# Two transformer blocks in one kernel: the first block's residual and norms on other engines, and one more slot for split weights

## The chip, the core and the metric

The kernel runs on one core of a Trainium2 chip. The metric is device time in microseconds, from one launch, as the median of three runs. A core has five engines with a queue of instructions each: TensorE (PE: products; PEld: its weight loads), VectorE (DVE), ScalarE (ACT), GpSimd (POOL) and SyncE (SP), on whose queue nearly all transfers are issued. Each engine works through its queue in order, and semaphores tie the queues together. TensorE's clock is granted at one of two levels, 2.4 GHz (1.00 in the profile's rows) or 1.2 GHz (0.50).

## What is computed

256 tokens of 1024 features, in float32, through two blocks of two layers each. The first block's layer is, twice:

```python
shift, scale, gate = ada_modulation(c, ada_w[layer, 0], ada_b[layer, 0])
h = x * (1.0 + scale) + shift
y = mixer_ab(h, ...) if layer % 2 == 0 else mixer_c(h, ...)
x = layer_norm(DN_ALPHA * x + gate * y, ln_g[layer, 0], ln_b[layer, 0])
shift, scale, gate = ada_modulation(c, ada_w[layer, 1], ada_b[layer, 1])
h = x * (1.0 + scale) + shift
y = squared_relu_mlp(h, mlp_w1[layer], mlp_w2[layer])
x = layer_norm(DN_ALPHA * x + gate * y, ln_g[layer, 1], ln_b[layer, 1])
```

So it has four halves (mixer, MLP, mixer, MLP), each of which ends in a layer norm of alpha x + gate y, with alpha the fourth root of 4. The second block (a gated recurrence, an MLP, latent attention, an MLP) has plain residual sums and RMS norms in place of it.

## The kernel before, in words

**Products.** A float32 product is made of three: each operand is cut into a high part (rounded) and a low part (the rest), and hi x hi, hi x lo and lo x hi are summed in PSUM (`mmA` at L219, `mmB` at L233; their lines L222 to L224 and L236 to L238 carry nearly all of TensorE's time). Tokens are in two tiles of 128, `t` = 0 and 1.

**Weights.** `Stream` holds all weights as items of 128 x 2048 float32 (1 MB) in the order of their use. A load (L122, on SP's queue) goes into one of four `raw` buffers. An item is then split in four pieces of 512 columns: ScalarE writes `whi` (L152), VectorE writes `wlo` = raw - whi (L153). The parts go into rings of `HL` = 6 tiles of 1024 columns each, which is room for three items. `hold` (L100) names items whose VectorE pieces are queued only behind a given instruction. Items of the adaLN modulation are in the stream as well: VectorE multiplies and sums them (`junk`, L421).

**MLP.** 16 hidden blocks; block j needs the items `(name, 1, j)` and `(name, 2, j)`. In the first block's two MLPs the first products of the blocks j = 0 and 1 run token tile by token tile (`head=2`), so that they can begin on tile 0.

**Between two halves** (`build`, L1684 to L1697; called a transition below). The last products of a half are held back in `fin(t)` (`tail`, L613). For each tile, `post_ln` (L533) does on VectorE: gate times y (L541), plus alpha x (L542), statistics (L543, L545); then the reciprocal root on GpSimd (L245, tile `rs`); then the normalized `xh`, two VectorE instructions of 128 x 512 (L551). `to_xT` (L270) transposes `xh` on TensorE (L279), ScalarE applies gain, scale and shift (L289), VectorE makes the high part `xTh` (L291) and the low part `xTl` (L292), with which the next half's products begin. After both tiles, `residual` (L594) makes alpha (xh g + b) for the next norm, on GpSimd: two instructions of 128 x 1024 a tile (L599, L600), into a new tile `xa`. `load_gb` (L581) loads the rows g and b; GpSimd multiplies them by alpha (L590, L591) except for the last norm. GpSimd also multiplies the first input by alpha (L1010), early in the kernel. `bcast_diag` (L436) puts a gate on all partitions.

**Order.** The program names engines and data; a planner with a cost model then puts each engine's instructions in an order, by the place in the program and by what it takes to be ready, and adds the semaphores. So what runs beside a transition may come from a later line of the program. A tile pool that opens after another has closed reuses its memory.

The four transitions: T0 (first mixer to first MLP, about 140 to 175 us of the profile), T1 (first MLP to second mixer, 340 to 380), T2 (second mixer to second MLP, 480 to 515), T3 (second MLP to the second block, 680 to 715).

Of the kernel before, what the change touches and what calls it, by code (L numbers as in the profile page):

```python
# [52 lines left out]
class Weights:  # L53
    """A chunk's hi and lo parts, in tiles that end at `cuts`"""
# [18 lines left out]
class Native:  # L73
    """A chunk as it is, in two tiles that meet at `cut`"""
# [10 lines left out]
class Stream:  # L85
    """Weights in the order of their use: loads run ahead, parts are split ahead."""

    def __init__(self, kb, load_ahead):
        self.kb = kb
        self.items = []  # L90
        self.index = {}
        self.nload = 0
        self.load_ahead = load_ahead
        self.queue = []
        self.nsplit = 0
        self.res = {}
        self.raw = {}
        self.held, self.behind = (), ()

    def hold(self, key, a, b, behind):  # L100
        """Items a to b after `key` are split behind these instructions"""
        i = self.index[key]
        self.held, self.behind = range(i + a, i + b), [x.ins if hasattr(x, "ins") else x for x in behind]

    def add(self, key, src, cols, cuts=None, gains=None, fn=None, step=512, f32=False):
        self.index[key] = len(self.items)
        self.items.append((key, src, cols, gains, fn, step, cuts, f32))

    def _load_to(self, i):
        kb = self.kb  # L110
        while self.nload <= min(i, len(self.items) - 1):
            key, src, cols = self.items[self.nload][:3]
            if self.items[self.nload][7]:
                # float32 products: into the split parts' place
# [11 lines left out]
    def _pieces(self, i):  # L126
# [17 lines left out]
        for a, b, g in gains:  # L144
            def pc(a=a, b=b, g=g):
                i, s = w.at(slice(a, b))
                if i == len(his):
                    his.append(kb.pw.tile([128, kb.HW], F32R, tag="whi", name=kb.nm("whi"), bufs=kb.HL))
                    los.append(kb.pw.tile([128, kb.HW], F32R, tag="wlo", name=kb.nm("wlo"), bufs=kb.HL))
# [12 lines left out]
    def pump(self, n=1, limit=None):  # L162
        """Emit up to n pieces; at most to item `limit`."""
# [28 lines left out]
class Kern:  # L192
# [33 lines left out]
    def mm(self, ps, x, w, c, start, stop):  # L226
        """x (hi, lo) with split weights, or one float32 operand with weights as they are"""
# [12 lines left out]
    def rsqrt(self, out, in_, mul, eps, n=1, pool=None):  # L240
        """out = (in * mul + eps) ** -0.5 on [128, n]"""
# [9 lines left out]
    def tm(self, name):  # L251
        """Token-major [128, 1024] scratch."""
        return self.px.tile([128, 1024], F32, tag="tm", name=self.nm(name), bufs=8)

    def split_evac(self, hi, lo, ps, gain=None):
        """hi + lo = ps (* gain), ps in PSUM"""
# [13 lines left out]
    def to_xT(self, x, t, xT, mode):  # L270
        """One token-major tile -> its columns of the feature-major hi/lo tiles.
        mode: None, (gain columns,) or (scale columns, bias columns)"""
# [54 lines left out]
    def setup_late(self):  # L327
        """Masks and rope tables"""
        nc, A, pc, c = self.nc, self.aps, self.pc, self.c
        nc.sync.dma_start(self.sink, A["rows"][ROWS["sinks"]:ROWS["sinks"] + 1, 0:8].to_broadcast([128, 8]))  # L330
        # bf16 identity and masks (added to the scores in PSUM)
# [13 lines left out]
        # rope tables of the second block: [cos | cos], [-sin | sin]  # L345
# [4 lines left out]
    def rope1_tables(self):  # L350
        """cos/sin of positions * inv, one [128, 64] each per token tile, sin signed [-sin | sin]."""
# [23 lines left out]
        # cos(r) = sin(r + pi/2), wrapped into [-pi, pi]  # L375
# [18 lines left out]
    def rope(self, out, src, nh, cos, sin):  # L394
        """out, src: [128, nh * 64]; src in PSUM"""
# [19 lines left out]
    def ada_piece(self, raw, j, acc, n):  # L415
        """acc[:, n] = sum_k raw[:, j, k] * silu(c)[k]"""
# [8 lines left out]
    def ada_bias(self, mod, acc, i, a, b):  # L425
        """mod = acc + b (+1 on scale and gate)"""
        self.nc.vector.tensor_tensor(mod[:, a:b], acc[:, a:b], self.adab[:, 24 * i + a:24 * i + b], op=ALU.add)

    def diag(self, cols):
        """Eight columns, each on the diagonal of a 128 x 128 block"""  # L430
# [5 lines left out]
    def bcast_diag(self, dst, d):  # L436
        """dst[128, 1024] = the blocks' diagonals along the free axis, on every partition"""
        nc = self.nc
        for g in range(2):
            p = self.ps("o")  # L440
            nc.tensor.matmul(p, self.ones, d[:, 4 * g:4 * g + 4, :].rearrange("p a b -> p (a b)"), start=True, stop=True)
            nc.scalar.activation(dst[:, g * 512:(g + 1) * 512], p, AF.Copy)

# [1 line left out]
    def attn_scores(self, t, heads, qk, mask, scale, sink=None, norm_act=False):  # L445
        """Scores and softmax of a few heads of one query tile.
        t = 0: 4 heads x 128 keys; t = 1: 2 heads x 256 keys.  Returns P (token-major)."""
# [43 lines left out]
    def attn_T(self, pt):  # L491
        """Transposed probabilities: four [128 keys, 128 queries] blocks."""
# [8 lines left out]
    def attn_pv(self, t, heads, pT, v, o, split=True):  # L501
        """o(h): PSUM region of head h; v(h, block): [128 keys, dv]"""
# [4 lines left out]
        elif split:  # L507
            # two column halves of the array side by side
# [10 lines left out]
    def attention(self, units, lag=2, hook=None):  # L519
        """units: list of (stage1 -> P, stage2(pT))"""  # L520
# [12 lines left out]
    def post_ln(self, acc, gate, xa, t):  # L533
        """One token tile: normalized alpha x + gate y, without the gain"""
# [12 lines left out]
        self.rsqrt(rs, ag[:, 1:2], 1.0, LN_EPS)  # L547
        x = self.tm("xh")
        for nb in range(2):
            sl = slice(nb * 512, nb * 512 + 512)  # L550
            self.ln_last = nc.vector.tensor_scalar(x[:, sl], r[:, sl], ag[:, 0:1], rs,  # L551
                                                   op0=ALU.subtract, op1=ALU.mult)
        return x

    def norm_in(self, li, gate):
        """Norm of layer half li and the next half's input, to be called for one token tile after the other"""
# [24 lines left out]
    def load_gb(self, li, scale):  # L581
        """Gain and bias rows of a norm on every partition, scaled"""
# [6 lines left out]
        if scale != 1.0:  # L589
            nc.gpsimd.tensor_scalar(g, g, scale, None, op0=ALU.mult)  # L590
            nc.gpsimd.tensor_scalar(b, b, scale, None, op0=ALU.mult)  # L591
        self.gb = (g, b)

    def residual(self, x):  # L594
# [1302 lines left out]
```

## Time and profile before

| | us |
|---|---|
| median of 3 runs | 1391.0 |
| lowest, highest run | 1390.44, 1391.79 |
| span of the profiled execution | 1393.9 |

The profiled execution gives no time of its own outside the span: from its first to its last instruction it took 1393.9 us, 2.9 us above the median of the timed runs. The page's table of engines has the busy time, the share of the span and the instructions of each engine. A row of the view by stretches gives the length of a stretch, then the busy time of PE, PEld, DVE, ACT and POOL with the instructions that began in it, TensorE's granted clock, the share of the transfer engines and GB/s. A row of the timeline gives start, length, engine, line, operation, out<-in with shapes, and how many instructions were merged; in brackets the idle time before, and who ended it. Consecutive instructions of one engine overlap by some 0.08 us.

### The profile page before, as it was taken

Reading aid. Unit: us, or ns where it says so; the run is one execution under the profiler, and the core shown is the slowest. Engines: PE = TensorE matmul, PEld = TensorE weight load, DVE = VectorE, ACT = ScalarE, POOL = GpSimd, SP = SyncE. Lnnn points to the kernel's source line nnn. Section 1 sums busy time; section 2 is a strip of 40 time slices with the busy share of each in tenths; the row PEclk is TensorE's granted clock in tenths of the full one; section 3 lists DMA queues with packets and bytes.
Section 4 is the critical chain, followed back from the end, with each engine's and each line's share of the span. In section 5 each row is a group of like instructions: output and inputs, shape, how many; then the busy total and the mean of one; then the engine's idle time right before and its main releaser. Section 6 shows DMA issues by size and latency. Waiting matters only on the chain.

```text
span 1393.9 us, 20506 instructions
## 1 busy us (share of the span) xinstructions
PE 1315.7 (94%) x7816; PEld 1114.9 (80%) x7822; DVE 987.2 (71%) x1862; ACT 697.4 (50%) x1490; POOL 110.1 (8%) x98
## 2 busy tenths in 40 slices
PE   5979799999799979999889999999999999999997
PEld 2446599988687669998679897999987987899996
DVE  7799898866998688555688787555558555655554
ACT  2257445544466445445453445444457764544552
POOL 3001400000400130000030000000001000000000
PEclk9989899999899989999979999999999999999999
DMA  9549398774375348555343423555544342355540
GB/s 367 218 159 354 103 373 320 286 276 152 127 296 214 119 138 315 184 185 179 119 168 118 152 92 121 181 181 181 184 168 177 122 151 92 136 182 187 191 166 31
DMA packets 38837, 260.16 MB, mean 187 GB/s; under 512 B 4562, under 2 KB 4818, under 8 KB 9171
## 3 DMA queue, kind: packets, MB, share of 16 engines
q1 hardware_dynamic: 38594, 258.34, 51.0%
q8 instruction: 61, 1.00, 0.3%
q0 software_dynamic: 144, 0.52, 0.1%
q14 instruction: 38, 0.30, 0.1%
HBM read 257.79 MB, written 1.05 MB: 186 GB/s over the span
## 4 chain that ended last, share of the span: by engine, by line
PE 80%; DVE 12%; issue 3%; ACT 2%; DMA 1%; POOL 1%; SPq 0%; DVEq 0%; POOLq 0%; ACTq 0%
PE acc L224 13%; PE acc L222 12%; PE acc L223 12%; PE scr L237 9%; PE scr L238 9%; PE scr L236 9%; DVE wlo L153 3%; PE scr L458 3%; DVE xh L551 1%; DMA raw<-in_ada_dram 1%; DVE junk L421 1%; PE o L496 1%; PE acc L1294 1%; PE o L1294 1%; POOL sm L245 1%
## 5 line engine op out<-in xcount | busy, mean ns | idle before, releaser
L153 DVE TENSOR_TENSOR wlo<-raw,whi 128x512 fp32r<-128x512 f32 x724 | 490.2, 710 | 287.4 <-ACT whi L152 274.5
L152 ACT ACTIVATE whi<-raw 128x512 fp32r<-128x512 f32 x724 | 421.5, 626 | 455.3 <-PE acc L224 202.6
L236 PE MATMUL scr<-xTh,whi 128*128 128x256 f32 x1088 | 310.5, 286 | 1.9 <-DVE xTh L291 1.9
L237 PE MATMUL scr<-xTl,whi 128*128 128x256 f32 x1088 | 309.2, 284 | 0.4 <-DVE xTl L292 0.2
L238 PE MATMUL scr<-xTh,wlo 128*128 128x256 f32 x1088 | 309.2, 284 | 0.0
L236 PEld LDWEIGHTS scr<-xTh,whi 128*128 128x128 f32 x1088 | 208.9, 192 | 5.2 <-DVE xTh L291 2.4
L237 PEld LDWEIGHTS scr<-xTl,whi 128*128 128x128 f32 x1088 | 209.0, 192 | 3.9 <-DVE xTl L292 0.9
L238 PEld LDWEIGHTS scr<-xTh,wlo 128*128 128x128 f32 x1088 | 209.1, 192 | 0.1
L222 PE MATMUL acc<-whi,hh 128*128 128x512 f32 x512 | 202.1, 395 | 0.0
L224 PE MATMUL acc<-whi,hl 128*128 128x512 f32 x512 | 201.8, 396 | 0.0
L223 PE MATMUL acc<-wlo,hh 128*128 128x512 f32 x512 | 201.7, 395 | 0.0
L421 DVE SCALAR_TENSOR_TENSOR junk<-raw,csil 128x1024 bf16<-128x1024 f32 x96 | 121.5, 1265 | 8.9 <-DMA raw<-in_ada_dram 7.9
L224 PEld LDWEIGHTS acc<-whi,hl 128*128 128x128 f32 x512 | 96.5, 188 | 22.9 <-DVE hl L695 0.8
L222 PEld LDWEIGHTS acc<-whi,hh 128*128 128x128 f32 x512 | 96.8, 189 | 20.4 <-ACT hh L693 1.1
L223 PEld LDWEIGHTS acc<-wlo,hh 128*128 128x128 f32 x512 | 96.5, 189 | 19.6
L245 POOL TENSOR_TENSOR sm<-rsq,mhalf 128x1 f32<-128x1 f32 (+2 forms) x26 | 19.7, 757 | 869.1 <-DVE rsq L244 869.1
L222 PE MATMUL acc<-whi,xTh 128*128 128x512 f32 (+1 forms) x176 | 67.0, 382 | 3.6 <-DVE xTh L291 3.6
L223 PE MATMUL acc<-wlo,xTh 128*128 128x512 f32 (+1 forms) x176 | 66.0, 375 | 2.0 <-DVE wlo L153 2.0
L224 PE MATMUL acc<-whi,xTl 128*128 128x512 f32 (+1 forms) x176 | 65.4, 372 | 1.4 <-DVE xTl L292 1.4
L692 ACT ACTIVATE r<-scr 128x512 f32<-128x512 f32 x60 | 35.0, 583 | 25.9 <-PE scr L238 25.9
L694 DVE TENSOR_TENSOR f<-r 128x512 f32<-128x512 f32 x60 | 41.1, 685 | 9.0 <-ACT r L692 8.9
L223 PE MATMUL scr<-wlo,xTh 128*128 128x256 f32 x128 | 40.7, 318 | 4.2 <-DVE wlo L153 4.0
(380 smaller groups left out, 1946.7 us busy)
## 6 DMA issues: line engine op xcount, KB each, us to landing
raw<-in_m_w_dram SPq DMA_DIRECT2D x128, 1024.0 KB, 4.8
raw<-in_ada_dram SPq DMA_DIRECT2D x48, 1024.0 KB, 5.2
raw<-in_c_qk_dram SPq DMA_DIRECT2D x8, 1024.0 KB, 4.7
raw<-in_h_qf_dram SPq DMA_DIRECT2D x8, 1024.0 KB, 4.8
raw<-in_mla_o_dram SPq DMA_DIRECT2D x8, 1024.0 KB, 4.8
raw<-in_c_v_dram SPq DMA_DIRECT2D x4, 1024.0 KB, 5.2
raw<-in_c_w_out_dram SPq DMA_DIRECT2D x4, 1024.0 KB, 5.3
raw<-in_h_i_dram SPq DMA_DIRECT2D x4, 1024.0 KB, 4.8
```

The lines of the kernel that those rows point to most:

```text
L152: nc.scalar.activation(hi, raw[:, a:b], AF.Copy)
L153: nc.vector.tensor_tensor(lo, raw[:, a:b], hi.bitcast(F32), op=ALU.subtract)
L222: mm(ps, xh, wh, start=start, stop=False)
L223: mm(ps, xh, wl, start=False, stop=False)
L224: mm(ps, xl, wh, start=False, stop=stop)
L236: mm(ps, wh, xh, start=start, stop=False)
L237: mm(ps, wh, xl, start=False, stop=False)
L238: mm(ps, wl, xh, start=False, stop=stop)
L421: nc.vector.scalar_tensor_tensor(junk, raw[:, j * 1024:(j + 1) * 1024], 1.0, self.csil, op0=ALU.mult, op1=ALU.mult, accum_out=acc[:, n:n + 1])
L458: nc.tensor.matmul(o, q, k, start=False, stop=(i == len(ops) - 1))
L692: nc.scalar.activation(r, p, AF.Relu)
L694: nc.vector.tensor_tensor(f, r, r, op=ALU.mult)
```

## The change

Five edits in the first block, one of which also reaches the second block's MLPs.

1. alpha is divided out of the norm: the gate is scaled by 1/alpha where it is put on all partitions, epsilon by 1/alpha^2, and x stays as it is. The GpSimd scalings of x, g and b go.
2. `post_ln` normalizes in place. VectorE does columns 0 to 511 and a small product `nm` = -mean rs; ScalarE does columns 512 to 1023 with `rs` and `nm`.
3. `residual` is done by VectorE, in eight instructions of 128 x 512 per transition, all queued behind the transition's last `xTl`. After T0 and T2 they stand in the program at hidden block j = 3 of the MLP, after T1 at the mixer's second group of heads, after T3 at once. `load_gb` in the MLPs moves from j = 2 to j = 4.
4. The MLP's items `(name, 1, j)` for odd j below 14 and `(name, 2, 15)` are split into a pool of their own with room for one item, in all four MLPs.
5. `hold` begins at the second item after the named one (before: the first), except in T1, and its instruction is now the first half's normalization.

```diff
-                    his.append(kb.pw.tile([128, kb.HW], F32R, tag="whi", name=kb.nm("whi"), bufs=kb.HL))
-                    los.append(kb.pw.tile([128, kb.HW], F32R, tag="wlo", name=kb.nm("wlo"), bufs=kb.HL))
+                    pool, n = (kb.pw2, 2) if key in self.extra else (kb.pw, kb.HL)
+                    his.append(pool.tile([128, kb.HW], F32R, tag="whi", name=kb.nm("whi"), bufs=n))
+                    los.append(pool.tile([128, kb.HW], F32R, tag="wlo", name=kb.nm("wlo"), bufs=n))
...
-            nc.scalar.activation(dst[:, g * 512:(g + 1) * 512], p, AF.Copy)
+            nc.scalar.activation(dst[:, g * 512:(g + 1) * 512], p, AF.Copy, scale=1.0 / ALPHA)
...
-        self.rsqrt(rs, ag[:, 1:2], 1.0, LN_EPS)
-        x = self.tm("xh")
-        for nb in range(2):
-            sl = slice(nb * 512, nb * 512 + 512)
-            self.ln_last = nc.vector.tensor_scalar(x[:, sl], r[:, sl], ag[:, 0:1], rs,
-                                                   op0=ALU.subtract, op1=ALU.mult)
-        return x
+        self.rsqrt(rs, ag[:, 1:2], 1.0, LN_EPS / (ALPHA * ALPHA))
+        nm = self.small(1, tag="nm")
+        self.ln_last = nc.vector.tensor_scalar(r[:, 0:512], r[:, 0:512], ag[:, 0:1], rs,
+                                               op0=ALU.subtract, op1=ALU.mult)
+        nc.vector.scalar_tensor_tensor(nm, ag[:, 0:1], -1.0, rs, op0=ALU.mult, op1=ALU.mult)
+        nc.scalar.activation(r[:, 512:1024], r[:, 512:1024], AF.Identity, scale=rs, bias=nm)
+        return r
...
-        if scale != 1.0:
-            nc.gpsimd.tensor_scalar(g, g, scale, None, op0=ALU.mult)
-            nc.gpsimd.tensor_scalar(b, b, scale, None, op0=ALU.mult)
...
-        o = self.tm("xa")
-        nc.gpsimd.tensor_tensor(o, x, g, op=ALU.mult)
-        nc.gpsimd.tensor_tensor(o, o, b, op=ALU.add)
-        return o
+        with self.tc.issue_after(after):
+            for x in xs:
+                for v, op in zip(gb, (ALU.mult, ALU.add)):
+                    for nb in range(2):
+                        sl = slice(nb * 512, nb * 512 + 512)
+                        nc.vector.tensor_tensor(x[:, sl], x[:, sl], v[:, sl], op=op)
...
-            S.add((name, 1, j), A[name + "_w1"][j], 2048)
+            S.add((name, 1, j), A[name + "_w1"][j], 2048, extra=j % 2 == 1 and j < 14)
...
-        S.add((name, 2, 15), A[name + "_w2"][15], 2048)
+        S.add((name, 2, 15), A[name + "_w2"][15], 2048, extra=True)
...
-                for t in range(2):
-                    nc.gpsimd.tensor_scalar(self.xtok[t], self.xtok[t], ALPHA, None, op0=ALU.mult)
-                self.load_gb(0, ALPHA)
+                self.load_gb(0)
...
+            if g == 1:
+                self.run_later()
...
-                xT, xh = trans(1)
-                xa = [self.residual(x) for x in xh]
+                xT, xa = trans(1)
                 first = [("m0", 1, 0), ("cqk", 0, 0), ("m1", 1, 0), ("hi", 0, 0)][li]
-                S.hold(first, 3 if li == 1 else 1, 5, [self.ln_last])
+                S.hold(first, 3 if li == 1 else 2, 5, [self.ln_last])
+                args = (xa, self.gb, self.xt_last.ins if hasattr(self.xt_last, "ins") else self.xt_last)
                 if li == 3:
+                    self.residual(*args)
                     break
+                self.later = [lambda args=args: self.residual(*args)]
...
-                        if j == 2:
-                            self.load_gb(li + 1, 1.0 if li == 2 else ALPHA)
+                        if j == 3:
+                            self.run_later()
+                        if j == 4:
+                            self.load_gb(li + 1)
...
-                    with tc.tile_pool(name="pml", bufs=1) as self.pm:
+                    with tc.tile_pool(name="pml", bufs=1) as self.pm, tc.tile_pool(name="pw2", bufs=1) as self.pw2:
```

## Rows read from the trace of the kernel before

**Rows 1.** Span and clock of the core, and the page's TensorE row.
```profile
core 0: 1393.9 us, clock 0.971
PE 1315.7 (94%) x7816; PEld 1114.9 (80%) x7822; DVE 987.2 (71%) x1862; ACT 697.4 (50%) x1490; POOL 110.1 (8%) x98
```

**Rows 2.** By stretches: the transitions T0 to T3.
```profile
140.00:175.00 35.00, 27.54 (x146) 21.19 (x145) 30.96 (x40) 14.41 (x36) 17.24 (x8) 0.80 0.32 112
340.00:380.00 40.00, 30.98 (x146) 25.06 (x145) 37.76 (x55) 14.80 (x33) 16.39 (x11) 0.83 0.35 122
480.00:515.00 35.00, 25.82 (x147) 23.12 (x146) 28.74 (x39) 14.58 (x35) 11.16 (x6) 0.80 0.30 110
680.00:715.00 35.00, 26.20 (x95) 18.98 (x94) 30.40 (x44) 15.99 (x35) 16.13 (x11) 0.76 0.25 94
```

**Rows 3.** By stretches: the four slow-clock stretches, first and last, and their sum.
```profile
155.59:169.24 13.65, 9.42 (x38) 8.19 (x39) 13.65 (x11) 3.01 (x8) 13.04 (x6) 0.50 0.24 68
...
694.90:711.96 17.06, 11.24 (x28) 7.92 (x29) 16.37 (x19) 6.24 (x14) 12.50 (x8) 0.50 0.23 86
sum 58.02, PE 38.80 PEld 32.15 DVE 56.25 ACT 16.31 POOL 41.01; mean PE 9.70 PEld 8.04 DVE 14.06 ACT 4.08 POOL 10.25
```

**Rows 4.** Timeline of TensorE around T0 and T3.
```profile
152.78 0.28 PE L222 MATMUL scr<-whi,xTh 128*128 128x256 f32 x1
156.28 1.09 PE L279 MATMUL o<-cst,xh 128*128 128x128 f32 x4 [3.22 <-DVE xh L551]
...
692.15 0.39 PE L224 MATMUL acc<-whi,xTl 128*128 128x512 f32 x1
692.37 0.39 PE L222 MATMUL acc<-whi,xTh 128*128 128x512 f32 x1
```

**Rows 5.** Timeline of VectorE: T0's tile 0, then its tile 1, then T3's tile 1.
```profile
144.00 1.00 DVE L551 TENSOR_SCALAR xh<-r,sm,sm 128x512 f32<-128x512 f32 x2 [0.69 <-POOL sm L245]
...
153.59 5.04 DVE L551 TENSOR_SCALAR xh<-r,sm,sm 128x512 f32<-128x512 f32 x2 [0.67 <-POOL sm L245]
158.54 6.21 DVE L153 TENSOR_TENSOR wlo<-raw,whi 128x512 fp32r<-128x512 f32 x3
...
694.59 5.04 DVE L551 TENSOR_SCALAR xh<-r,sm,sm 128x512 f32<-128x512 f32 x2 [0.66 <-POOL sm L245]
```

**Rows 6.** Timeline of GpSimd in T0: first and last of its four residual instructions.
```profile
153.51 2.34 POOL L599 TENSOR_TENSOR xa<-xh,gbc 128x1024 f32<-128x1024 f32 x1
...
161.51 2.68 POOL L600 TENSOR_TENSOR xa<-xa,bbc 128x1024 f32<-128x1024 f32 x1
```

**Rows 7.** By stretches: the sum over each transition before tile 1's norm is ready.
```profile
sum 54.30, PE 51.12 PEld 37.30 DVE 44.23 ACT 27.98 POOL 5.70; mean PE 12.78 PEld 9.33 DVE 11.06 ACT 6.99 POOL 1.43
```

**Rows 8.** Timeline of VectorE and ScalarE: tile 0 of T2, from norm to split input.
```profile
484.24 1.00 DVE L551 TENSOR_SCALAR xh<-r,sm,sm 128x512 f32<-128x512 f32 x2 [0.69 <-POOL sm L245]
485.60 2.90 ACT L289 ACTIVATE aff<-o,sm,sm 128x128 f32<-128x128 f32 x8 [0.59 <-PE o L279]
487.13 0.43 DVE L291 CAST xTh<-aff 128x512 fp32r<-128x512 f32 x1 [1.29 <-ACT aff L289]
488.08 0.68 DVE L292 TENSOR_TENSOR xTl<-aff,xTh 128x512 fp32r<-128x512 f32 x1
```

**Rows 9.** One line's instructions: ScalarE with a per-token scale; durations min/median/max in ns.
```profile
L1229 ACT ACTIVATE hv<-acc,sm x4: 671/688/692, 712.0 to 787.5; 128x512 f32<-128x512 f32 x4
```

**Rows 10.** Timeline: VectorE's splits in the first MLP, and TensorE's use of them.
```profile
211.80 4.30 DVE L153 TENSOR_TENSOR wlo<-raw,whi 128x512 fp32r<-128x512 f32 x7
...
214.74 0.28 PE L236 MATMUL scr<-xTh,whi 128*128 128x256 f32 x1
214.86 0.28 PE L237 MATMUL scr<-xTl,whi 128*128 128x256 f32 x1
```

**Rows 11.** By stretches: the first MLP's start, and the second mixer.
```profile
175.00:200.00 25.00, 25.00 (x157) 22.41 (x156) 23.84 (x40) 12.29 (x25) 0.00 (x0) 1.00 0.98 384
...
170.00:230.00 60.00, 60.00 (x390) 54.65 (x389) 57.25 (x94) 31.32 (x62) 3.10 (x2) 1.00 0.89 340
375.00:440.00 65.00, 64.74 (x385) 52.59 (x385) 60.52 (x132) 40.30 (x100) 0.00 (x0) 1.00 0.78 289
```

**Rows 12.** By stretches: two transitions of the second block.
```profile
860.00:870.00 10.00, 8.47 (x44) 6.38 (x43) 7.96 (x18) 7.50 (x24) 1.66 (x2) 0.95 0.34 113
1197.00:1207.00 10.00, 7.92 (x45) 6.44 (x44) 9.36 (x21) 9.25 (x24) 1.09 (x2) 1.00 0.19 75
```

More of the change, by code (lines that the diff above doesn't have):

```diff
@@ L98, in __init__ @@
         self.held, self.behind = (), ()
+        self.extra = set()
     def hold(self, key, a, b, behind):
@@ L103, in hold, with add @@
         self.held, self.behind = range(i + a, i + b), [x.ins if hasattr(x, "ins") else x for x in behind]
-    def add(self, key, src, cols, cuts=None, gains=None, fn=None, step=512, f32=False):
+    def add(self, key, src, cols, cuts=None, gains=None, fn=None, step=512, f32=False, extra=False):
         self.index[key] = len(self.items)
         self.items.append((key, src, cols, gains, fn, step, cuts, f32))
+        if extra:
+            self.extra.add(key)
     def _load_to(self, i):
@@ L579, in norm_in, with load_gb @@
         return half, trans
-    def load_gb(self, li, scale):
+    def load_gb(self, li):
         nc = self.nc
@@ L588, in load_gb, with residual, run_later @@
         nc.sync.dma_start(b, R[ROWS["ln_b"] + li:ROWS["ln_b"] + li + 1, :].to_broadcast([128, 1024]))
-        if scale != 1.0:
-            nc.gpsimd.tensor_scalar(g, g, scale, None, op0=ALU.mult)
-            nc.gpsimd.tensor_scalar(b, b, scale, None, op0=ALU.mult)
         self.gb = (g, b)
-    def residual(self, x):
+    def residual(self, xs, gb, after):
         nc = self.nc
-        g, b = self.gb
-        o = self.tm("xa")
-        nc.gpsimd.tensor_tensor(o, x, g, op=ALU.mult)
-        nc.gpsimd.tensor_tensor(o, o, b, op=ALU.add)
-        return o
+        with self.tc.issue_after(after):
[4 more added lines that the diff above has]
+                        nc.vector.tensor_tensor(x[:, sl], x[:, sl], v[:, sl], op=op)
+    def run_later(self):
+        for f in self.later:
+            f()
+        self.later = []
     def mod_cols(self, mod, li):
@@ L1122, in mixer_c @@
         acc = [[self.ps("acc") for _ in range(2)] for _ in range(2)]
-        self.load_gb(2, ALPHA)
+        self.load_gb(2)
         parts = []
@@ L1722, in build @@
         h, xT, r1, r2 = self.resid_step(acc, h, None, (self.col("mlp_norm", 0, 8),))
-        with tc.tile_pool(name="pml2", bufs=1) as self.pm:
+        with tc.tile_pool(name="pml2", bufs=1) as self.pm, tc.tile_pool(name="pw3", bufs=1) as self.pw2:
             acc = self.mlp("m2", xT)
@@ L1728, in build @@
         h, xT, r1, r2 = self.resid_step(acc, h, None, (self.col("mlp_norm", 8, 8),))
-        with tc.tile_pool(name="pml3", bufs=1) as self.pm:
+        with tc.tile_pool(name="pml3", bufs=1) as self.pm, tc.tile_pool(name="pw4", bufs=1) as self.pw2:
             fg = self.pm.tile([128, 1024], F32, tag="fg", name="fg")
```

## The prediction

> **What bounds the kernel.** I read the page's engine rows first: TensorE is busy for 1315.7 of 1393.9 us, and the core's mean granted clock is 0.971 [rows 1]. So TensorE is the bound, and two things can be gained: the idle time, and the time at the lower clock. Next, the view by stretches. In the MLPs there is nothing to gain (60.00 us busy of 60 [rows 11]). The loss sits at the four transitions, where 35, 40, 35 and 35 us hold 27.54, 30.98, 25.82 and 26.20 us of TensorE [rows 2]: 7.46 + 9.02 + 9.18 + 8.80 = 34.46 us idle. In each there is also one stretch at 0.50, from 13.65 to 17.06 us long, together with 38.80 us of busy TensorE [rows 3]; at 1.00 that work would take half, so 19.40 us are lost to the clock. Sum 53.9 us, some 12 to 14 at each transition (T0: 7.46 + 9.42/2 = 12.2; T3: 8.80 + 11.24/2 = 14.4).
>
> Third, the timelines of the engines say why. In T0 the normalization of tile 0 takes 1.00 us for its two halves, while that of tile 1 takes 5.04 [rows 5]. The difference is GpSimd: from 153.51 it runs the residual's first instruction, of 2.34 us [rows 6], in just the time of tile 1's two halves (from 153.59). The three split pieces behind them take 6.21 us instead of about 1.9, as GpSimd goes on to 164; undisturbed, seven take 4.30 [rows 10], so 0.61 each. TensorE has run dry by then (3.22 us idle, released by `xh` L551 [rows 4]), starts the transposes, waits for more, and its clock drops at 155.59. T3 shows the same 5.04 [rows 5]. Before tile 1's norm there is little: those stretches together hold 51.12 us of TensorE in 54.30 [rows 7], an idle of 3.2.
>
> **The change, part by part.**
>
> *Residual off GpSimd, VectorE's two slow halves gone.* The loss of 53.9 is removed, except for what stays even in an undisturbed transition.
>
> (a) 3.2 us before tile 1's norm: not touched [rows 7].
>
> (b) The second half of the norm on ScalarE. The trace has no such instruction; ScalarE with a per-token scale on 128x512 takes 0.69 [rows 9], from PSUM, against 0.5 for VectorE's half. It starts as late as `nm`, a small instruction behind VectorE's half. With VectorE's second half ending 1.0 after `rs` and ScalarE's at about 1.3, it costs 0.3 per transition, 4 x 0.3 = 1.2. Bounds: 0 (VectorE's two halves were the later ones) to 0.8 each, 3.2, if ScalarE is queued behind one 0.69 split.
>
> (c) The wait between `rs` and tile 1's first products, which needs work from elsewhere. Tile 0 of T2 shows the chain undisturbed: norm at 484.24, `xTh` done at 487.13 + 0.43 = 487.56, `xTl` at 488.76 [rows 8]; so 3.3 and 4.5 us behind the norm's start, 3.6 and 4.8 with (b). What TensorE has in this time: the second block of w1 is no longer held back and has a place of its own, so its products on tile 0 can run. In T0 these are 24 products of 256 columns at 0.12 [rows 10], 2.9 us; with eight transposes (four take 1.09 at the low clock [rows 4], so some 0.11 to 0.14 each, 0.9 in all) it is dry some 1.4 us. In T3 the next products are 12 of 512 columns at 0.23 [rows 4], 2.8 us, of which part is run before `rs`: some 2.6 us dry. For T1 and T2 I take 2.0 each. Sum 1.4 + 2.0 + 2.0 + 2.6 = 8.0. Bounds: 4 (the planner finds other work) to 12 (none of the un-held products is ready).
>
> (d) The clock. If idle per transition is 3 us instead of 8 to 9, does it still fall? Two transitions of the second block have like gaps: 1.53 us idle in 860 to 870 at a clock of 0.95, and 2.08 idle in 1197 to 1207 at 1.00 [rows 12]. I take it as staying up, and leave the other case as a rival.
> The Trainium skill (TensorE: Matmul & The Clock Gate, Part 1: The HAM clock gate) says that the low clock is the state of rest, lifted by activity, and that the point where it changes varies from run to run. By that, the same gap can cost differently in each execution, and (d) would be a matter of chance rather than of the gap's length. The rows neither show nor exclude it: slow stretches of 13.65 to 17.06 us belong to four different transitions of one execution [rows 3]. Against much of chance speaks that the three timed runs, with their stretches, lie within 1.35 us.
>
> So 3.2 + 1.2 + 8.0 = 12.4 us stay, and the gain here is 53.9 - 12.4 = 41.5.
>
> *The residual on VectorE.* 32 instructions of 128x512, eight a transition. The like instruction, a split piece, has a pitch of 0.61 [rows 10]: 4.9 us of VectorE in each of the places. They are queued behind the last `xTl`, which is long done there; so nothing waits in front of them, but all VectorE work behind them is later by up to 4.9.
> First MLP: TensorE is fully busy, and VectorE has 57.25 of 60 us [rows 11]. What covers the residual is the lead of the splits: the pieces from 211.80 are used from 214.74, so about 3 us [rows 10]. To this comes the VectorE time that the transition gives back, 5.04 - 1.00 + 6.21 - 1.9 = 8.3 us [rows 5]. I take 0.5; without this cover, 4.9 + 1 = 5.9. The transfers there are at 0.98 of their engines from 175 to 200 [rows 11]; they wait for raw buffers that the splits empty, so they move forward with the splits, and I take nothing for them.
> Second mixer: VectorE has 60.52 of 65 us and TensorE 64.74 [rows 11]; little room, and its short chains run over VectorE, so 3 of the 4.9 (0 to 6.2, with the idle of 4.48 unable to take any).
> T3: the residual comes at once and the second block's first norm reads it: 1 (0 to 4.9).
> Second MLP: VectorE has room, 0.
> Sum 4.5, bounds 0 to 17.0.
>
> *The extra slot.* A w1 item of odd blocks no longer queues for the ring. Its part in the gain is in (c). Its room is one item, so the next odd block's pieces wait for this one's last product: two blocks later, each (48 x 0.12 + 24 x 0.23) = 11.3 us, enough for four pieces of 0.61. Nothing.
>
> *Everything else.* The scalings of x, g, b by GpSimd, the load of g and b at j = 4 (two transfers on SP's queue, in a half with TensorE at 60.00 of 60 [rows 11]), the gate's scale in an existing ScalarE instruction, epsilon: no time on TensorE's path. Without cover, `nm` would be one small VectorE instruction per tile, and is in (b).
>
> **Sum.** 41.5 - 4.5 = 37.0. The profiled span 1393.9 becomes 1356.9; it lies 2.9 above the median of the runs, and 1391.0 - 37.0 = 1354.0.
>
> **The rivals.**
>
> B: the clock still falls. Idle goes as in the sum, but in two to four transitions a stretch like those of [rows 3] remains. For: 0.95 with only 1.5 us idle [rows 12]. Against: 1.00 with 2.1. Each costs 38.80/8 = 4.85: two give 1354 + 9.7 = 1364, four 1373. The skill's rule above would make this likelier, not larger.
>
> C: VectorE becomes the bound. It gets 19.6 us of work in places where it has 57.25 of 60 and 60.52 of 65 [rows 11]; then the upper bounds hold: 17.0 - 4.5 = 12.5 more, 1366.5.
>
> E: the change doesn't do what it says. With the hold beginning one item later, four pieces (2.4 us) get in front of VectorE's norm in each transition; the idle comes back (9.8) and with it all clocks (19.4): 41.5 - 9.8 - 19.4 - 4.5 = 7.8, 1383. Against: the planner puts work by its place in the program, and the norm is due at once.
>
> D, slower: the single place for odd w1 items. The six later odd blocks of each of four MLPs, 24 in all, can be split only when the previous one's last product is done. If the split came just before use, each would cost four pieces and a ScalarE one, 4 x 0.61 + 0.69 = 3.1, in all 74 us: 1354 + 74 = 1428. It decides from 37/24 = 1.5 us a block. Against: the place is free for a whole block (11.3 us) before the next use; for: VectorE's full queue in the first MLP [rows 11].
>
> **Chances.** Forecast 0.60 (its own range 1347 to 1361), B 0.17, C 0.10, E 0.05, no change 0.03, D 0.05. About 0.2%, 2.8 us, is what a measurement of this kernel can tell from no change. Range: down to 1354 - 4.5 (residual hidden) - 4 (c at 4) - 1.2 (b at 0) = 1344; up to 1354 + 19.4 (B, all four) + 2.6 (a fifth of C with it) = 1376. Faster: 0.60 + 0.17 + 0.10 + 0.05 = 0.92; same 0.03; slower 0.05.
>
> **What would show it.** In the profile after: VectorE's halves of the norm at 0.5 us for both tiles, no residual on GpSimd, 32 of it on VectorE near 0.69 each; granted clock 1.00 through the four transitions, mean near 0.999; about 3 us idle in each, TensorE's busy time about 1315.7 - 19.4 = 1296. TensorE still 60 of 60 in the first MLP, else C; idle ahead of odd blocks on `whi` or `wlo`, then D. Slow stretches beside small gaps mean that (d) failed. The sum is wrong if TensorE's idle in a transition is above 5 us, or the second mixer loses more than 6.

## The result and the profile after

The changed kernel takes 1355.5 us as the median of four runs (1353.08 to 1357.5), against 1391.4 for the kernel before, run beside it: a ratio of 0.9739, 95% interval 0.9724 to 0.9754. Forecast were 1354.0 us, in a range of 1344 to 1376. The profiled execution took 1354.8 us from first to last instruction, 39.1 less than that of before [rows 1]. A run's time lies some 1.8 us above its span (1356.6 for this one), so the profiled execution of before, with its 1393.9, was one of the longer ones.

The core's line and the rows of two engines on the page of the kernel after (busy time, share of the span, instructions):

```profile
core 0: 1354.8 us, clock 0.987
...
PE 1300.2 (96%) x7816; PEld 1103.7 (81%) x7822; DVE 962.7 (71%) x1894; ACT 703.1 (52%) x1498; POOL 43.8 (3%) x74
```

GpSimd's 110.1 us [rows 1] are now 43.8. VectorE has 32 instructions more and is yet busy for 24.5 us less: it does the residual's work (22 us), but half of the norm has gone to ScalarE, and the rest of its work is no longer slowed by GpSimd's residual.

The same four transitions by stretches (length, then busy PE, PEld, DVE, ACT, POOL, TensorE's granted clock, transfer share, GB/s), with their sum:

```profile
140.00:175.00 35.00, 31.58 (x180) 25.04 (x179) 30.53 (x59) 22.43 (x51) 1.10 (x2) 0.95 0.64 232
330.00:370.00 40.00, 37.61 (x192) 31.53 (x190) 35.90 (x66) 19.13 (x41) 5.30 (x7) 0.96 0.46 163
460.00:495.00 35.00, 31.61 (x190) 27.30 (x189) 30.98 (x57) 20.15 (x46) 1.10 (x2) 0.95 0.59 208
650.00:685.00 35.00, 32.51 (x166) 26.17 (x165) 29.41 (x56) 20.25 (x43) 6.36 (x7) 0.95 0.29 100
sum 145.00, PE 133.30 PEld 110.04 DVE 126.83 ACT 81.95 POOL 13.86; mean PE 33.32 PEld 27.51 DVE 31.71 ACT 20.49 POOL 3.46
```

TensorE's idle time falls from 34.46 us [rows 2] to 145.00 - 133.30 = 11.70. The clock still falls, once in each transition, but shortly. The four stretches at 0.50, by the same view (the first, and the sum):

```profile
159.01:162.42 3.41, 3.28 (x15) 3.28 (x16) 3.41 (x8) 0.74 (x2) 0.00 (x0) 0.50 0.83 279
...
sum 13.64, PE 13.32 PEld 12.37 DVE 13.33 ACT 5.95 POOL 0.00; mean PE 3.33 PEld 3.09 DVE 3.33 ACT 1.49 POOL 0.00
```

They hold 13.32 us of products, where there were 38.80 [rows 3]; 6.7 us are lost to the clock instead of 19.4. Idle and clock together: 53.9 before, 18.4 after, so 35.5 of the 39.1 us were gained here.

What is left can be read from VectorE's timeline in T0, at tile 1 (in brackets the idle time before, and who ended it):

```profile
153.96 0.55 DVE L555 TENSOR_SCALAR r<-r,sm,sm 128x512 f32<-128x512 f32 x1 [0.66 <-POOL sm L250]
154.42 0.15 DVE L557 SCALAR_TENSOR_TENSOR sm<-sm,sm 128x1 f32<-128x1 f32 x1
154.49 2.49 DVE L158 TENSOR_TENSOR wlo<-raw,whi 128x512 fp32r<-128x512 f32 x4
156.91 0.43 DVE L296 CAST xTh<-aff 128x512 fp32r<-128x512 f32 x1
157.25 1.22 DVE L426 SCALAR_TENSOR_TENSOR junk<-raw,csil 128x1024 bf16<-128x1024 f32 x1
158.39 0.09 DVE L426 DVE_READ_ACCUMULATOR junk<-raw,csil 128x1 f32 x1
158.39 0.69 DVE L297 TENSOR_TENSOR xTl<-aff,xTh 128x512 fp32r<-128x512 f32 x1
```

The norm's half takes 0.55 us, the split pieces 0.62 each; both stood at 2 to 2.5 [rows 5]. But between `xTh` and `xTl` a sum of the modulation (`junk`) has come in, and TensorE waits for it:

```profile
157.39 0.39 PE L227 MATMUL scr<-whi,xTh 128*128 128x256 f32 x1 [0.95 <-DVE xTh L296]
...
159.14 0.58 PE L229 MATMUL scr<-whi,xTl 128*128 128x256 f32 x1 [1.00 <-DVE xTl L297]
```

In T1 another GpSimd instruction has taken the residual's place beside the norm, the gate's spreading on a diagonal (L437). GpSimd's and VectorE's timelines:

```profile
347.05 0.55 POOL L250 TENSOR_TENSOR sm<-rsq,mhalf 128x1 f32<-128x1 f32 x1 [4.22 <-DVE rsq L249]
347.57 1.90 POOL L437 TENSOR_TENSOR diag<-cst,adamod 128x1024 f32<-128x1024 f32 x1
```

```profile
347.64 2.11 DVE L555 TENSOR_SCALAR r<-r,sm,sm 128x512 f32<-128x512 f32 x1 [0.73 <-POOL sm L250]
```

VectorE's half begins 0.07 us behind it and ends 0.28 us after it.

The two kinds of instruction that are new, ScalarE's half of the norm and the moved residual, by their lines (durations min/median/max in ns), and the halves that the residual is moved into, by stretches:

```profile
L558 ACT ACTIVATE r<-r,sm,sm x8: 813/814/817, 145.4 to 668.1; 128x512 f32<-128x512 f32 x8
...
L605 DVE TENSOR_TENSOR r<-r,gbc x16: 684/690/695, 177.9 to 675.8; 128x512 f32<-128x512 f32 x16
L605 DVE TENSOR_TENSOR r<-r,bbc x16: 683/687/692, 180.0 to 677.0; 128x512 f32<-128x512 f32 x16
```

```profile
170.00:230.00 60.00, 60.00 (x374) 53.92 (x373) 58.33 (x97) 29.92 (x55) 2.72 (x1) 1.00 0.87 327
365.00:430.00 65.00, 64.28 (x395) 53.09 (x396) 62.43 (x132) 37.19 (x94) 0.00 (x0) 1.00 0.69 250
```

The first MLP stays full; the second mixer has 0.72 us of idle TensorE in 65, against 0.26 [rows 11].

### The profile page after: what moved, and what is told of

The parts are those of the page before. It is cut to its first block, busy times and chain, and to the rows that moved or that the text cites. A ratio compares the mean times of both kernels' runs of the same rounds, so it can differ in the third digit from the quotient of the medians.

```text
span 1354.8 us, 20530 instructions
## 1 busy us (share of the span) xinstructions
PE 1300.2 (96%) x7816; PEld 1103.7 (81%) x7822; DVE 962.7 (71%) x1894; ACT 703.1 (52%) x1498; POOL 43.8 (3%) x74
## 4 chain that ended last, share of the span: by engine, by line
PE 81%; DVE 11%; ACT 3%; DMA 2%; issue 1%; POOL 1%; SPq 0%; DVEq 0%; POOLq 0%; ACTq 0%
PE acc L227 13%; PE acc L229 13%; PE acc L228 12%; PE scr L242 10%; PE scr L243 10%; PE scr L241 9%; PE scr L463 2%; DVE wlo L158 2%; DMA raw<-in_ada_dram 2%; DVE junk L426 1%; PE o L501 1%; PE acc L1303 1%; PE o L1303 1%; POOL sm L250 1%; PE scr L229 1%
## 5 line engine op out<-in xcount | busy, mean ns | idle before, releaser
L158 DVE TENSOR_TENSOR wlo<-raw,whi 128x512 fp32r<-128x512 f32 x724 | 474.1, 691 | 271.7 <-ACT whi L157 260.8
L426 DVE SCALAR_TENSOR_TENSOR junk<-raw,csil 128x1024 bf16<-128x1024 f32 x96 | 118.6, 1236 | 6.5 <-DMA raw<-in_ada_dram 5.9
L228 PE MATMUL acc<-wlo,xTh 128*128 128x512 f32 (+1 forms) x176 | 63.1, 360 | 0.0
L476 ACT ACTIVATE pt<-scr,sm 128x128 f32<-128x128 f32 (+1 forms) x96 | 39.2, 420 | 7.6 <-DVE sm L468 5.3
```

Of the source, the lines that this page charges most:

```text
L158: nc.vector.tensor_tensor(lo, raw[:, a:b], hi.bitcast(F32), op=ALU.subtract)
L228: mm(ps, xh, wl, start=False, stop=False)
L426: nc.vector.scalar_tensor_tensor(junk, raw[:, j * 1024:(j + 1) * 1024], 1.0, self.csil, op0=ALU.mult, op1=ALU.mult, accum_out=acc[:, n:n + 1])
L476: nc.scalar.activation(pt[:, j * nk:(j + 1) * nk], s[:, j * nk:(j + 1) * nk], AF.Exp, scale=scale, bias=ng[:, j:j + 1], accum_out=sm[:, j: ...
```

## The experiments

The theory is that of the prediction: GpSimd's residual slows VectorE at tile 1's norm, TensorE runs dry, its clock falls. The rivals: the other edits carry the gain (the un-held w1 block, the slot, ScalarE's half); and, of the theory itself, whether it is GpSimd's work as such or its place that costs.

### One edit alone, or one undone

**The residual alone**, in the kernel before:

```diff
-                xT, xh = trans(1)
-                xa = [self.residual(x) for x in xh]
+                xT, xa = trans(1)
...
+                self.later = [lambda args=args: self.residual(*args)]
```

> The kernel before with edit 3 alone: the residual in place on VectorE behind the last xTl, at the places of the change; norm, slot, hold and the scalings by alpha as before. Theory (GpSimd's residual slows VectorE at tile 1's norm): most of the gain is here. The two halves of tile 1's norm fall from 5.04 to about 1.0 us, the split pieces from 2.07 to 0.62 each; without un-held work TensorE idles 4 to 5 us a transition, so 1361 us (1355 to 1368). Rival (the gain is the un-held second w1 block that fills TensorE's gap): 1385 us or more.

Measured: 1359.3 us, ratio 0.9763 (0.9748 to 0.9777). VectorE's timeline in T0 (two halves, then three pieces) shows the slowing nearly gone, and the sum of the four transitions by stretches, each as long as above, shows TensorE's idle time at 145.00 - 128.84 = 16.2 us:

```profile
152.69 1.71 DVE L551 TENSOR_SCALAR xh<-r,sm,sm 128x512 f32<-128x512 f32 x2 [0.66 <-POOL sm L245]
154.33 2.72 DVE L153 TENSOR_TENSOR wlo<-raw,whi 128x512 fp32r<-128x512 f32 x3
```

```profile
sum 145.00, PE 128.84 PEld 105.43 DVE 129.99 ACT 76.20 POOL 23.31; mean PE 32.21 PEld 26.36 DVE 32.50 ACT 19.05 POOL 5.83
```

Of the 2.6% of the whole change, 2.4 are here. Which edit carries the rest is not shown: the division by alpha was not tried alone, nor the slot and the hold undone together. GpSimd still scales g and b in this kernel, and in T0 it does so beside tile 1's norm:

```profile
152.63 2.78 POOL L590 TENSOR_SCALAR gbc<-gbc 128x1024 f32<-128x1024 f32 x1
```

Of the norm's 1.71 us the first half has 1.26 and the second 0.54.

**The slot and the later hold alone**, in the kernel before (the edits to `_pieces`, `mlp_items` and `S.hold` of the change, nothing else):

> The kernel before with edits 4 and 5 alone: the slot for odd w1 items and the hold from the second item; the residual stays on GpSimd in the transition. Theory: VectorE's halves still take 5.04 us, TensorE gets at most 2.9 us more work a transition, and the clock still falls: 1385 us (1378 to 1391). Rival (un-held work is the gain): 1362 us or less.

Measured: 1394.4 us, ratio 1.0009 (0.9999 to 1.0018). No gain, and 1394 is above the 1378 to 1391 that even the theory gave it. VectorE at tile 1 of T0:

```profile
154.50 5.04 DVE L555 TENSOR_SCALAR xh<-r,sm,sm 128x512 f32<-128x512 f32 x2 [0.67 <-POOL sm L249]
159.46 6.19 DVE L157 TENSOR_TENSOR wlo<-raw,whi 128x512 fp32r<-128x512 f32 x3
```

The same 5.04 and 6.2 as in [rows 5]. More ready work for TensorE was worth nothing while VectorE was held up.

**The slot undone**, in the kernel after (`extra` false throughout, all tiles from the ring of six):

> The changed kernel without edit 4: all items in the ring of six tiles, the hold as changed. Theory (the slot is worth the un-held products of (c), some 2 to 3 us in T0, T2 and T3): 1361 us (1357 to 1366). Rival D (a single place delays odd blocks, so the slot costs): 1355 us or less. If the slot carries the gain: 1375 us or more.

Measured: 1355.7 us, ratio 0.9733 (0.9717 to 0.9749). The same as the whole change, so no worth of the slot is shown. A small one isn't excluded: this kernel's runs have mean clocks of 0.989 to 0.994 against the change's 0.987 to 0.992, and at 0.992 it took 1356.8 us where the change took 1353.1 and 1354.4. Rival D, which would have made a slot of one item the cause of a slower kernel, falls.

**The hold undone**, in the kernel after (`3 if li == 1 else 1` for `... else 2`):

> The changed kernel with the hold from the first item again, so that the second w1 block is split only behind tile 1's norm. As predicted in (c), its products on tile 0 are missing in TensorE's gap, 2.9 us in T0 and T2 and 2.8 in T3, and the clock falls for longer: 1364 us (1360 to 1368). Rival (other products fill the gap, as the kernel without the slot suggests): 1358 us or less.

Measured: 1355.7 us, ratio 0.9717 (0.9697 to 0.9738). By its time the rival holds: no worth of the second w1 block's products is shown. The profiled execution is less plain. TensorE idles 2.35 us in T0, where it idled 3.42, but in T3 5.83 of 35, where it idled 2.49:

```profile
648.00:683.00 35.00, 29.17 (x138) 23.19 (x137) 29.69 (x58) 18.52 (x39) 6.98 (x7) 0.95 0.22 81
```

The residual alone, with the same hold, has 6.12 there. So in T3 the un-held item does fill the gap, by some 3 us; over all four transitions the profile has 13.99 us of idle time, against 11.70.

**The split norm undone**, both halves on VectorE:

```diff
-        nc.vector.scalar_tensor_tensor(nm, ag[:, 0:1], -1.0, rs, op0=ALU.mult, op1=ALU.mult)
-        nc.scalar.activation(r[:, 512:1024], r[:, 512:1024], AF.Identity, scale=rs, bias=nm)
+        self.ln_last = nc.vector.tensor_scalar(r[:, 512:1024], r[:, 512:1024], ag[:, 0:1], rs,
+                                               op0=ALU.subtract, op1=ALU.mult)
```

> The changed kernel with both halves of the norm on VectorE, 0.55 us each, and no nm; ScalarE then begins with gain and shift when the first four transposes are done. Theory (b): ScalarE's half delays its eight gain-and-shift instructions by 0.2 to 0.3 us a tile, so 1354.5 us (1352.5 to 1356). Rival (VectorE is the scarcer engine in the transition, and half a microsecond more of it delays the split pieces and xTl): 1357 us or more.

Measured: 1356.2 us, ratio 0.9736 (0.9719 to 0.9753), against 0.9739: no difference that the runs can tell, so by the times neither side of (b) is shown. The traces lean to the rival: in T0 the first `xTh` of tile 1 begins 3.32 us behind the norm's start here and 2.95 in the kernel after, as VectorE's four split pieces start later; the four transitions idle for 13.2 us, against 11.7.

### The residual on GpSimd again, in two places

**At once**, with all other edits:

```diff
-                        nc.vector.tensor_tensor(x[:, sl], x[:, sl], v[:, sl], op=op)
+                nc.gpsimd.tensor_tensor(x, x, v, op=op)
...
+                self.residual(*args)
```

> The changed kernel with the residual back on GpSimd, in place and at once behind each transition, as four instructions of 128x1024; all other edits stay. Theory: it meets tile 1's norm or the splits and transposes behind it; the norm's half on VectorE goes from 0.55 to about 2.5 us, the clock falls for 10 us or more in each transition: 1382 us (1374 to 1392). Rival (the other four edits carry the gain): 1360 us or less.

Measured: 1393.6 us, ratio 1.0003 (0.9992 to 1.0013), so the whole gain is lost. It went beyond the 1382 that was expected, and by another meeting than the one expected: the residual of tile 0 starts behind that tile's norm and transposes, at 147.02, and not beside tile 1's norm (153.51 in [rows 6]). Why the order is another was not tested. GpSimd and VectorE in T0, at tile 0:

```profile
147.02 2.34 POOL L602 TENSOR_TENSOR r<-r,gbc 128x1024 f32<-128x1024 f32 x1 [2.40 <-ACT r L558]
149.44 2.42 POOL L602 TENSOR_TENSOR r<-r,bbc 128x1024 f32<-128x1024 f32 x1
```

```profile
147.59 2.05 DVE L296 CAST xTh<-aff 128x512 fp32r<-128x512 f32 x1 [1.73 <-ACT aff L294]
149.56 2.85 DVE L547 TENSOR_TENSOR r<-lnt,xt 128x512 f32<-128x512 f32 x1
```

The norm's half is at 0.55 here, contrary to the expectation; the cast of `xTh` takes 2.05 us instead of 0.43, and the sum for tile 1's norm 2.85 instead of 0.69. Each VectorE instruction ends 0.28 to 0.55 us after the GpSimd instruction that it met, as if it had waited for the end of it.
The Trainium skill (SBUF — State Buffer, Who interferes with whom) says just this: the two engines share a pair of ports under an exclusive lock, and of two instructions that both need it, the second to start is blocked until the first is done. The trace agrees, with 2.05 and 2.85 here and 2.11 in T1 of the kernel after. All three met a `tensor_tensor` of GpSimd. Beside its scaling, a `tensor_scalar`, the residual alone shows less: the norm's first half, begun 0.06 us behind GpSimd, is done at 153.95, 1.5 us ahead of GpSimd's end. There the wait is not the whole instruction, and the measurement decides.

**Later.** A first attempt, with the residual on GpSimd at the program's later places, did not part place from engine:

> The changed kernel with the residual on GpSimd again, but at the later places and behind the last xTl. It parts place from engine. If GpSimd's sharing costs VectorE time wherever it runs: four instructions of some 2.5 us each slow the split pieces beside them from 0.61 to 2.07 us, some 7 us of VectorE in each half; with VectorE at 58 of 60 us in the first MLP and 62 of 65 in the second mixer, 1366 us (1361 to 1374). If only the place in the transition costs: 1358 us or less.

Measured: 1391.1 us, ratio 0.9986 (0.9974 to 0.9997). The later place acts on the order of one engine's queue only; GpSimd had nothing else to do, and ran the residual at 146.92, as at once. So this run says no more than the one before it. In the second attempt GpSimd waits for data that VectorE makes at the later place:

```diff
+            nc.vector.tensor_copy(gb[0][:, 0:1], gb[0][:, 0:1])
             for x in xs:
                 for v, op in zip(gb, (ALU.mult, ALU.add)):
+                    nc.gpsimd.tensor_tensor(x, x, v, op=op)
```

> The changed kernel with the residual on GpSimd, this time truly late: its first operand g also depends on a one-column VectorE copy that stands where the changed kernel's residual stands. It parts place from engine. If only the transition is a bad place: VectorE loses some 7 us in each half to sharing, against 4.9 for doing the work itself, and most of it is hidden as the 4.9 are: 1357 us (1354 to 1361). If GpSimd's sharing costs wherever it runs: 1366 us or more.

Measured: 1373.7 us, ratio 0.9858 (0.9836 to 0.9881), so by its time the second: sharing costs at the later places as well. But not at all of them. By stretches, where GpSimd's residual now runs (second mixer, second MLP, second block, and last the first MLP):

```profile
375.00:395.00 20.00, 15.51 (x76) 11.87 (x75) 20.00 (x39) 8.42 (x26) 8.36 (x3) 0.83 0.54 204
485.00:505.00 20.00, 15.58 (x81) 13.78 (x81) 16.99 (x22) 9.90 (x25) 10.76 (x4) 0.77 0.46 158
685.00:705.00 20.00, 14.38 (x85) 13.08 (x84) 17.63 (x19) 11.36 (x20) 15.57 (x9) 0.81 0.45 172
172.00:232.00 60.00, 60.00 (x375) 53.96 (x374) 59.56 (x86) 29.93 (x55) 14.94 (x5) 1.00 0.84 320
```

In the first MLP VectorE is busy for 59.56 of 60 us and TensorE loses nothing. In the three others 4.4 to 5.6 us of each 20 are idle, and the clock falls; of like stretches in the kernel after, the second mixer's (365 to 385) and the second block's (672 to 692) lose none and the second MLP's (478 to 498) 1.39. In the second mixer TensorE waits 2.21 and 2.28 us for VectorE's `cqkr` (the first takes 2.84 us, undisturbed 0.69), in the second MLP 3.20 for `hl`, which stands behind three split pieces of 2.1 each. Behind T3 it is another thing: TensorE waits 4.98 us for `dg`, an instruction of GpSimd, which needs the second block's norm of the residual, and the residual takes 10.8 us there, where VectorE took 4.9. That is the residual's own length on the path. So GpSimd's sharing costs where the next product hangs on VectorE's next instructions, and nothing where VectorE works on splits that are needed later.

### The price of the residual on VectorE, and a faster order

**Without the residual:**

> The changed kernel without the residual: the eight VectorE instructions per transition are left out, so the next norm adds the plain normalized x. It prices the 4.5 us that the prediction gave back. By the trace after, TensorE is busy for 60.00 of 60 us in the first MLP, so theory now: nearly all hidden, 1354 us (1352 to 1356). As predicted (0.5 + 3 + 1): 1351. Rival C (VectorE bounds there): 1345 us or less.

Measured: 1353.7 us, ratio 0.9721 (0.9704 to 0.9739), against 0.9739: 1.8 thousandths, some 2.5 us; the intervals overlap, so no price is shown. The second mixer, by stretches:

```profile
365.00:430.00 65.00, 64.72 (x392) 53.09 (x393) 59.72 (x130) 37.84 (x93) 0.00 (x0) 1.00 0.70 262
```

TensorE is idle for 0.28 us there, against 0.72 with the residual.

**xTl first.** What stood between `xTh` and `xTl` is queued behind `xTl`:

```diff
-                S.hold(first, 3 if li == 1 else 2, 5, [self.ln_last])
+                S.hold(first, 3 if li == 1 else 2, 6, [self.ln_last, self.xt_last], 0 if li == 1 else 1)
```

The last argument is the number of items that stay behind the norm's half (in T1 none); the others, three, are behind the last `xTl` (the expectation says five).

> The changed kernel with only one held item behind the norm's half and the next five behind the transition's last xTl, so that no sum of the modulation and no split piece stands between VectorE's xTh and xTl. Theory (these 1.2 us in T0 and 0.6 in T2 are on TensorE's path): 1353.5 us, 1352 where the clock then stays up. Rival (the pieces that go behind come late for TensorE): 1357 us or more.

Measured: 1350.3 us, ratio 0.9694 (0.9676 to 0.9711), clear of the change's 0.9724 to 0.9754. In its profiled execution the clock is at 1.00 in all four transitions, and their sum is:

```profile
sum 145.00, PE 134.66 PEld 112.22 DVE 128.24 ACT 83.20 POOL 14.82; mean PE 33.67 PEld 28.05 DVE 32.06 ACT 20.80 POOL 3.71
```

So of the 8.1 us between the two profiled executions only 1.4 are idle time (10.34 against 11.70); 6.7 are what the clock's falls took there. That the order keeps the clock up is not shown by this: in the profiled execution without the slot, with the old order and the same wait of 1.00 us for `xTl` in T0, it stayed at 1.00 in T0, T1 and T2.

**And in T1 the gate's spreading later:**

```diff
+                            with tc.issue_after(args[2]):
+                                nc.vector.tensor_copy(c2, cols)
```

> The changed kernel with the order of the run before (one item behind the norm's half, five behind the last xTl), and in T1 the spread gate on GpSimd fed from a copy that VectorE makes behind the last xTl, so that it no longer runs beside tile 1's norm. Theory (sharing again: there the norm's half took 2.11 us and not 0.55, and TensorE idled 1.8): the half falls to 0.55, the idle to 0.5, 1348.5 us (1346 to 1350.5). Rival (the spread gate comes late for the second mixer's end, or costs as much beside the rope): 1351 us or more.

Measured: 1349.8 us, ratio 0.9686 (0.9667 to 0.9704). The transitions by stretches:

```profile
140.00:175.00 35.00, 32.48 (x200) 26.01 (x198) 31.49 (x60) 21.19 (x48) 1.10 (x2) 1.00 0.62 231
330.00:370.00 40.00, 39.09 (x204) 32.23 (x203) 35.53 (x69) 19.00 (x42) 3.43 (x6) 1.00 0.43 167
...
sum 145.00, PE 136.29 PEld 113.53 DVE 128.07 ACT 83.40 POOL 12.96; mean PE 34.07 PEld 28.38 DVE 32.02 ACT 20.85 POOL 3.24
```

and VectorE's half at tile 1 of T1:

```profile
345.67 0.55 DVE L555 TENSOR_SCALAR r<-r,sm,sm 128x512 f32<-128x512 f32 x1 [0.73 <-POOL sm L250]
```

The mechanism is as expected (0.55 instead of 2.11, T1's idle time 0.91 instead of 2.39). That it adds to the run before is not shown: the intervals overlap widely. Both kernels beat the change, by some 0.5%.

## Why the prediction was right

**What bounds, and the cause.** Held. The residual moved alone gives a ratio of 0.9763, the whole change 0.9739, and put back on GpSimd it takes everything away (1.0003).

**(a), 3.2 us before tile 1's norm.** Held. The same parts of the transitions, up to tile 1's norm, have 3.5 us of idle time in the profile after (60.30 us of TensorE in 63.83).

**(b), ScalarE's half, 1.2 us.** No such cost was found: with both halves on VectorE the ratio is 0.9736. The instruction was under-priced, 0.81 us where I went by the 0.69 of [rows 9], and still its chain is not late: with VectorE doing both halves, the first `xTh` of T0's tile 1 begins later (3.32 us behind the norm's start, against 2.95).

**(c), 8.0 us idle.** The sum was right, in part by luck, and its reason was not the whole. All idle time of the transitions is 11.7 us, where (a), (b) and (c) gave 12.4. Behind the start of tile 1's norm it is 2.4, 1.8, 2.5 and 1.5 us in T0 to T3, where I had put 1.4, 2.0, 2.0 and 2.6. T0's 1.4 does not follow from its own terms either: 4.8 - 2.9 - 0.9 is 1.0. T1's comes from GpSimd's spreading of the gate, which I did not have at all. I took the un-held second block as what fills the gap, at 2.8 to 2.9 us a transition. By time no such worth is shown (without its slot 0.9733, with it held 0.9717); by the trace the un-held item fills some 3 us in T3 and nothing in T0, where TensorE idles 2.35 us with it held, 3.42 in the kernel after and 2.52 with `xTl` first. What I left out is VectorE's order behind the norm, foreign work between `xTh` and `xTl`. Queuing that later gives 0.9694 against 0.9739, by the profiles mostly by way of the clock.

**(d), the clock stays up.** This failed. It fell in all four transitions of the profiled execution, each time for 3.41 us, at a cost of 6.7 us: rival B's mechanism with a third of B's price a stretch (1.7 for 4.85), as the stretches are shorter. The size of such a fall stood in the trace of before. The first row of [rows 12], with 1.53 us of idle time and a clock of 0.95, ends just after the clock has fallen. The whole stretch at 0.50 is:

```profile
868.98:872.39 3.41, 3.41 (x17) 3.41 (x17) 2.72 (x6) 2.19 (x6) 0.45 (x1) 0.50 0.00 0
```

At 1.00 its 3.41 us of products would take half, so it costs 1.7 us, and four like it 6.8. I priced B by the long stretches of [rows 3] instead. The clock also varies. Of the four runs, two have a mean granted clock of 0.987 and took 1356.6 and 1357.5 us, two have 0.992 and took 1354.42 and 1353.08. Where in the runs that difference lies is not on record, as only one was profiled. I had held against this the closeness of three runs of the kernel before; its runs beside the experiments are less close (1389.9 to 1397.6 us).
The Trainium skill (TensorE: Matmul & The Clock Gate, Part 1: The HAM clock gate), which says that the point of change varies from run to run, was the better guide at this step. The runs agree in so far as one kernel has two levels of the mean clock, some 3 us apart.

**The give-back, 4.5 us.** Over-priced, as far as the runs can tell: by the two ratios it is some 2.5 us, with intervals that overlap. In the second mixer, to which I had given 3, the residual makes 0.44 us of idle time (0.72 against 0.28); the first MLP is full, as forecast.

**The sum.** Against the profiled execution I forecast 37.0; it was 39.1. In the transitions 35.5 us were gained where I had 41.5: the clock took 6.7, and the idle time came out 0.7 better. Outside them 3.6 were gained where I gave back 4.5, and nothing in the prediction accounts for that. Part of it may be chance at the kernel's start: up to 130 us the granted clock is 0.93 in the profiled execution of before and 0.95 in that of the kernel after, and 0.92 to 0.97 in those of the experiments on it, whose edits lie later. Against the medians the gain was 35.9, as the profiled execution of before, with a mean clock of 0.971 [rows 1], was a long one: of the runs of before beside the experiments, those with 0.970 or 0.971 took 1394.2 to 1397.6 us, those with 0.973 to 0.975 took 1390.3 to 1395.8, and those with 0.976 took 1389.9 to 1393.1. The forecast missed the median by 1.5 us, less than each of the larger terms was wrong by. The cause was right; that the time came so close is luck.

**Rivals.** B: came in part, with small stretches. C: VectorE does not bound in the halves (60.00 of 60). D: not there. E: the change does what it says, but a trace of E's thought is in the kernel, foreign VectorE work in the chain, only behind the norm and not before it.

## What to carry to other kernels

Work that GpSimd does "for free" beside a short VectorE chain can cost most of each GpSimd instruction (here 1.6 to 2.2 us beside a `tensor_tensor` of 1.9 to 2.4); look at the duration of VectorE's instructions there, not at who is idle, and give GpSimd only stretches where VectorE is ahead. When a chain is on the path, look at what stands between its links on the same engine: here queuing what stood between `xTh` and `xTl` behind them (a sum in T0, a split piece in T2) brought more than an extra buffer slot or a later hold was shown to bring. And where gaps lower TensorE's clock in some executions and not in others, compare several, since one profile shows only one of the outcomes.

## What was unexpected of the hardware

The clock falls at gaps that are far shorter than those of before: in T0 of the kernel after there are 0.95 and 1.00 us of idle time with 0.75 us of products between them, it falls at 159.01, within the second, and it comes back after 3.41 us. In the profiled execution of the kernel with `xTl` first it did not fall, though T0 and T2 have a gap of 0.95 us each, T3 one of 1.20 and T1 one of 1.80. That kernel's runs have mean clocks from 0.990 (1351.28 us) to 0.995 (1348.42). In T1 of the kernel after, it fell behind a gap of 1.81, hardly another. What decides it in one execution is open.

Also unexpected was that 12 us of GpSimd's work in the first MLP cost nothing at all, though three kinds of VectorE instructions there took 2.6 to 3.4 us. In the second mixer, the second MLP and behind T3 the same work goes with idle time and a lower clock, and that kernel is some 17 us slower than the change by the two ratios.
